# One way to take a mean: replacing the two-matmul norm sums by one-column matmuls in a conformer and attention trunk

## The chip, the cores and the metric

The kernel runs on one core of a Trainium2 chip. The metric is the device time of one execution in microseconds (us), the median of several runs. A core has a matrix engine (TensorE, PE in the profile, with its weight loads as PEld), a vector engine (VectorE, DVE), an activation engine (ScalarE, ACT), a general engine (GpSimd, POOL) and SyncE (SP), which here issues most of the DMAs. Each engine has its own instruction stream and works through it in the order written at build time; between engines there are only semaphores.

## The reference

A trunk of two layers over 512 tokens of width 1024, in float32. Each layer is a half-step SwiGLU feed-forward stage, a mixer (layer 0 a Conformer convolution, layer 1 a sparse attention), a second half-step feed-forward stage, and a gated embedding of a per-layer input p (ple). Each of the four starts with an RMS norm, and one more stands at the end.

```python
def rms_norm(x, g):
    xf = x.astype(jnp.float32)
    y = xf * lax.rsqrt(jnp.mean(xf * xf, axis=-1, keepdims=True) + RMS_EPS)
    return (y * g.astype(jnp.float32)).astype(x.dtype)

def swiglu(x, wg, wu, wd):
    return (jax.nn.silu(x @ wg) * (x @ wu)) @ wd

for i in range(DEPTH):                      # DEPTH = 2
    x = x + 0.5 * swiglu(rms_norm(x, ffn1_norm[i]), ffn1_w_gate[i], ffn1_w_up[i], ffn1_w_down[i])
    h = rms_norm(x, mix_norm[i])
    x = x + (conformer_conv(h, ...) if i % 2 == 0 else nsa_mixer(h, ...))
    x = x + 0.5 * swiglu(rms_norm(x, ffn2_norm[i]), ffn2_w_gate[i], ffn2_w_up[i], ffn2_w_down[i])
    gate = jax.nn.sigmoid(rms_norm(x, ple_norm[i]) @ ple_w_gate[i])
    x = x + gate * (p[i] @ ple_w_in[i])
return rms_norm(x, final_norm)
```

The width of a feed-forward stage is 2816.

## The kernel before

**Layout.** The activations are kept transposed: `self.xs[k]`, k = 0 to 7, each hold 128 of the 1024 channels as partitions and the 512 tokens as columns. Weights arrive in units of 128 x 1024 floats, loaded by SP into `raw` (or `rawx`) tiles of which there are two each. Every float32 operand of a product is split into a high half (`h`, a copy in a reduced format, made by ACT) and a low half (`l`, the difference, made by DVE or POOL): for weights these are `wh` and `wl` (L280, L281), for activations the pairs made in `parts` (L387, L388). A product is three matmuls: `mm3` (L329 to L331) computes high x high, high x low and low x high. All products accumulate in eight PSUM banks.

**The norm.** The norm's gain goes into the activation's split; the norm's factor r, one number for each token, is applied after the matmuls to their result, since it is the same for all channels. So a stage's matmuls can start before r is known. `square_sum` squares each of the eight tiles on ACT and adds them up on DVE in `acc` (L404), 128 partitions x 512 tokens. What remains is a sum over the 128 partitions for each token, a small addition of 1e-6, a power of -0.5 (on POOL, `rsqrt`, L410), and the spreading of r over the 128 partitions, which PE does by four transposes (`spread_raw`, L442) with a copy by ACT to `R` (L449).

`rfin` makes these steps as a generator with two stops: the first `next(fin)` writes down everything to r, the second one the spread. It has two ways of summing over the partitions:

- `soon=True`, used by the two mixers (`conv`, `cmp_in`): `token_sums` (L417) makes four matmuls with 128 columns of `acc` as the stationary operand and one column of 1/1024 as the moving one. The result has the tokens as partitions, 128 x 4. Each of the four float32 matmuls is two instructions in the trace.
- `soon=False`, used by the four feed-forward stages (`ffn`) and the two gates (`ple`): `acc` is split into `h` (ACT, L457) and `l` (DVE, L458), two tiles of the small ring of work tiles (`tmp`, four of them in these stages). `token_means` multiplies a 128 x 128 matrix of 1/1024 by both (L434, two 512-wide matmuls), which gives the mean of every token on every partition, and `diagonal` reads the wanted 128 x 4 numbers out of the bank by four multiply-and-reduce operations with the identity on DVE (L426, each with a read of its accumulator). Then comes the addition (L436).

**A feed-forward stage.** The 22 tiles of the hidden width go in three parts (`PARTS`). The first two tiles (f = 0 and 1) are computed plainly: eight products for the gate, eight for the up half each. From f = 2 on the gate of two tiles is computed together by `gate_pair`, with seven products of half size in the place of eight; these need sums and differences of weight blocks (`combine`, L292 to L304, on DVE and ACT) and of activation blocks. The latter are made once a stage by `right_sums`, called four times (two calls after f = 0, two after f = 1): two scaled copies by ACT (L482), four differences of 256 columns on DVE, and for two results a copy by ACT (L492) and a difference on DVE (all DVE ones at L484). It uses four work tiles a call; its results are the `px` tiles. The third of the seven products is the first to read them.

The calls of `fin` in `ffn`: the first after the products of f = 0, the second between the gate and the up products of f = 1. The multiplications by `R` (L575) come behind f = 1.

**What sets the order.** The order on each engine's stream is chosen at build time by a planner: it follows the order in which the program writes the instructions, but takes a later instruction when it reckons that an earlier one isn't ready yet. `tc.high_priority(100)` (`FIN_PRI`) lets what is written in its block count as written 100 instructions earlier. `tc.issue_after(ins)` demands that what its block writes on the engine of `ins` stands behind `ins` in that engine's stream; it adds no wait for its end. `conv` uses it already to put the tap building of POOL behind the power. `self.root` there is the power's instruction.

Of the kernel before, what the change touches and what calls it, by code (L numbers as in the profile page):

```python
# [11 lines left out]
F32 = mybir.dt.float32  # L12
F32R = mybir.dt.float32r
I32 = mybir.dt.int32
AF = mybir.ActivationFunctionType
OP = mybir.AluOpType
# [10 lines left out]
FIN_PRI = 100  # L27
# [158 lines left out]
class Kern:  # L186
# [230 lines left out]
                self.nc.tensor.matmul(p[:, q:q + 1], t[:, q * 128:q * 128 + 128], self.mean[:, :1],  # L417
                                      start=n == 0, stop=n == len(tiles) - 1)

    def diagonal(self, src, tag, n=4):  # L420

        nc = self.nc
        v = self.tiny.tile([128, 4], F32, name=tag, tag=tag)[:, :n]
        junk = self.cpool.tile([128, 128], F32, name="junk", tag="junk", bufs=1)
        for q in range(n):
            nc.vector.tensor_tensor_reduce(out=junk, in0=src[:, q * 128:q * 128 + 128], in1=self.ident, scale=1.0,  # L426
                                           scalar=0.0, op0=OP.mult, op1=OP.add, accum_out=v[:, q:q + 1])
        return v

    def token_means(self, acc, eps):  # L430
        nc = self.nc
        p = self.bank()
        for n, t in enumerate(acc):
            nc.tensor.matmul(p, self.meanr, t, start=n == 0, stop=n == 1)  # L434
        v = self.diagonal(p, "v")
        nc.vector.tensor_scalar(v, v, eps, None, op0=OP.add)  # L436
        return self.rsqrt(v, 4)

    def spread_raw(self, r, n=4):
        p = self.bank()[:, :n * 128]  # L440
        for q in range(n):
            self.nc.tensor.transpose(p[:, q * 128:q * 128 + 128], r[:, q:q + 1].to_broadcast([128, 128]), self.ident)  # L442
        return p
# [5 lines left out]
        nc.scalar.activation(R, p, AF.Copy)  # L449
        return R  # L450

    def rfin(self, acc, soon=False):


        if not soon:
            h, l = self.tmp(F32R), self.tmp(F32R)
            self.nc.scalar.activation(h, acc, AF.Copy)  # L457
            self.nc.vector.tensor_tensor(l, acc, h.bitcast(F32), op=OP.subtract)  # L458

        def steps():  # L460
            with self.tc.high_priority(FIN_PRI):
                if soon:
                    p = self.bank()[:, :4]
                    self.token_sums(p, [acc])
                    v = self.tiny.tile([128, 4], F32, name="v", tag="v")
                    self.nc.vector.tensor_scalar(v, p, 1e-6, None, op0=OP.add)
                    r = self.rsqrt(v, 4)
                else:
                    r = self.token_means((h, l), 1e-6)
            yield  # L470
            self.R = self.spread(r)
            yield

        return steps()


    def right_sums(self, name, i, k):
# [58 lines left out]
    def ffn(self, n, i, nxt):  # L536
        nc = self.nc
        X = self.X
        g, u, d = (f"ffn{n}_w_{s}" for s in ("gate", "up", "down"))
        self.now, self.T4 = (g, i), []  # L540
        fin = self.rfin(self.acc)

        def plain(p, nm, f, ks=range(KD)):
            for k in ks:
                self.mm3(p, self.block((nm, i, k, f)), X[k], k == 0, k == KD - 1)

        for pi, fs in enumerate(PARTS):
            hid = {}

            def gated(f, gr, pu):  # L550
                nc.vector.tensor_tensor(pu, pu, gr, op=OP.mult)  # L551
                h, l = self.ptile("hid", HIDS, dt=F32R), self.ptile("hid", HIDS, dt=F32R)
                nc.scalar.activation(h, pu, AF.Copy)
                nc.vector.tensor_tensor(l, pu, h.bitcast(F32), op=OP.subtract)
                hid[f] = (h, l)

            if pi == 0:
                assert PLAIN == 2
                wait = []
                for f in range(PLAIN):  # L560
                    pg, pu = self.bank(), self.bank()
                    for ks in (range(KD - 1), (KD - 1,)) if f == 0 else (range(KD),):
                        plain(pg, g, f, ks)
                        if f == 1:
                            next(fin)
                        plain(pu, u, f, ks)
                    wait.append((f, pg, pu))
                    if f == 0:
                        next(fin)
                    for k in (2 * f, 2 * f + 1):  # L570
                        self.right_sums(f"ffn{n}_norm", i, k)
                R = self.R
                for f, pg, pu in wait:
                    gr = self.tmp()
                    nc.vector.tensor_tensor(pg, pg, R, op=OP.mult)  # L575
                    nc.scalar.activation(gr, pg, AF.Silu)
                    gated(f, gr, pu)
            for f in fs[::2]:
                if f < PLAIN:
                    continue  # L580
                G = self.gate_pair(g, i, f)
                nc.vector.tensor_tensor(G, G, R[:, None, :].to_broadcast([128, 2, 512]), op=OP.mult)
                nc.scalar.activation(G, G, AF.Silu)
                for h in range(2):
                    p = self.bank()
                    plain(p, u, f + h)
                    gated(f + h, G[:, h], p)
                self.skew_next()
                self.skew_next()
            last = pi == len(PARTS) - 1  # L590
            if last:
                self.prep_start(*nxt)
            for ms in ((0, 1), *((m,) for m in range(2, KD))):
                p = {m: self.bank() for m in ms}
                if len(ms) > 1:
                    self.held = {ENTRY[PLACE[d, i, f, m][0]] for f in fs for m in ms}
                for part in (fs[:-2], fs[-2:]):
                    for m in ms:
                        for f in part:
                            self.mm3(p[m], self.block((d, i, f, m)), hid[f], f == fs[0], f == fs[-1])  # L600
                self.held = set()
                for m in ms:
                    nc.vector.scalar_tensor_tensor(p[m], p[m], 0.5, R, op0=OP.mult, op1=OP.mult)  # L603
                    nc.vector.tensor_tensor(self.xs[m], p[m], self.xs[m], op=OP.add)
                    if last:
                        self.prep(m)
# [192 lines left out]
    def conv(self, nxt):  # L799

        nc = self.nc
# [3 lines left out]
        self.dwc = self.phase.tile([128, KD, TAPS], F32, name="dwc")  # L805
        nc.gpsimd.dma_start(self.dwc, self.a["dwc"])
        self.ud, self.yd = (self.dpool.tile([D, S], F32, name=n) for n in ("ud", "yd"))
        fin = self.rfin(self.acc, True)
        self.T, self.late, self.done, self.mid, self.squares, self.sqp = {}, [], [], None, None, SQP
        work = {"dve": self.dw_dve, "pool": self.dw_pool, "pe": self.dw_pe}  # L810
        queues = {on: [] for on in work}
# [63 lines left out]
        with self.tc.high_priority(FIN_PRI):  # L875
# [4 lines left out]
            v = self.tiny.tile([128, 4], F32, name="v", tag="v")  # L880
# [3 lines left out]
            r = self.rsqrt(v, 4)  # L884
# [7 lines left out]
        for c in range(KD):  # L892
            pair = self.ptile("tw", TWB, 128 * LAGS, F32R)
            h, l = pair[:, :512], pair[:, 512:1024]
# [144 lines left out]
    def cmp_in(self, j, first):  # L1039

        nc = self.nc
        KC, wait = {}, []
        if first:
            fin = self.rfin(self.acc, True)
        for gp in range(2):
            p = self.bank()
            for k in range(KD):
                self.mm3(p, self.block(("nsa_w_in", 0, k, ("c", j, gp))), self.X[k], k == 0, k == KD - 1)
            wait.append((gp, p))
            if first and gp == 0:  # L1050
                next(fin)
        if first:
            self.proj_gates()
            next(fin)
        for gp, p in wait:
            for s in range(2):
                t = self.ptile("e", EB, 516)
                o = 1 - s
                sl, ot = slice(s * 64, s * 64 + 64), slice(o * 64, o * 64 + 64)
                nc.vector.tensor_tensor(t[sl, o:o + 512], p[sl], self.R[sl], op=OP.mult)  # L1060
                nc.sync.dma_start(t[ot, s:s + 512], t[sl, o:o + 512])
                KC[gp * 2 + s] = t
        B = []
        for q4 in range(4):
            b = self.slot()
            bv = b[:, :496].rearrange("p (a n) -> p a n", a=4)
            for g in range(G):
                src = KC[g][:, 1:1 + 512].rearrange("p (c q e) -> p q c e", q=8, e=2)
                pp0 = q4 * 4
                in0 = src[:, pp0 % 8:pp0 % 8 + 4, pp0 // 8:pp0 // 8 + NC, 0]  # L1070
                nc.gpsimd.tensor_tensor(bv[:, :, g * NC:g * NC + NC], in0,
                                        self.pos[:, j, pp0:pp0 + 4, None].to_broadcast([128, 4, NC]), op=OP.add)
            B.append(bv)
        return B
# [400 lines left out]
```

## Time and profile before

| | |
|---|---|
| runs | 2115.99, 2112.11, 2112.36 us; median 2112.36 |
| the profiled execution's own time | 2111.71 us |
| its span | 2109.9 us |
| mean granted TensorE clock | 0.983 |
| norms with the two-matmul sums, sums of squares done at | 19.4 us (first feed-forward stage), 586.8 (second), 951.4 (ple), 1000.6 (third feed-forward stage), 1695.8 (fourth), 2054.0 (ple) |
| norms with one-column sums, the same | 380.7 us (convolution), 1363.2 (attention) |
| HBM read, written | 203.25 MB, 16.29 MB |

How to read the profile's rows. A row of a timeline is: start and duration in us, engine, line of the kernel, operation, output tile <- input tiles, shapes, count, and in brackets how long the engine had been idle and what released it. A row of stretches is: the stretch, its length, busy time of PE, PEld, DVE, ACT and POOL with the number of instructions in brackets, then the granted clock of TensorE as a share of the full one, the busy share of the DMA engines and GB/s. A row of waits is: who waited for whom, us in total, times, the longest in us. A row of a line's instructions gives the shortest, the middle and the longest duration in ns, and when the first and the last one started. A row of groups gives count, busy us and mean ns. Matmuls overlap, so the pace of a stream of them is read from the distance of their starts.

### The profile page before, as it was taken

Reading aid. Unit: us, or ns where it says so; the run is one execution under the profiler, and the core shown is the slowest. Engines: PE = TensorE matmul, PEld = TensorE weight load, DVE = VectorE, ACT = ScalarE, POOL = GpSimd, SP = SyncE. Lnnn points to the kernel's source line nnn. Section 1 sums busy time; section 2 is a strip of 40 time slices with the busy share of each in tenths; the row PEclk is TensorE's granted clock in tenths of the full one; section 3 lists DMA queues with packets and bytes.
Section 4 is the critical chain, followed back from the end, with each engine's and each line's share of the span. In section 5 each row is a group of like instructions: output and inputs, shape, how many; then the busy total and the mean of one; then the engine's idle time right before and its main releaser. Section 6 shows DMA issues by size and latency. Waiting matters only on the chain.

```text
span 2109.9 us, 29020 instructions
## 1 busy us (share of the span) xinstructions
PE 2041.1 (97%) x11048; PEld 1762.0 (84%) x11048; DVE 1431.8 (68%) x2538; ACT 937.9 (44%) x1538; POOL 382.0 (18%) x388
## 2 busy tenths in 40 slices
PE   7999999999989999999899999999999989999998
PEld 6888888888768898988788989787888768898987
DVE  8757566796576665666856656646989785675664
ACT  6424234653553242345532423326888653242343
POOL 0000000785200000021000000446666200000022
PEclk8999999999999999999999999999999999999999
DMA  4323323344273233243233323454333133332241
GB/s 162 111 89 100 101 80 104 94 132 162 90 200 121 80 105 96 81 147 102 80 110 90 110 83 97 155 163 111 86 86 101 36 100 100 94 107 90 90 140 50
DMA packets 77339, 223.52 MB, mean 106 GB/s; under 512 B 8624, under 2 KB 16592, under 8 KB 77200
## 3 DMA queue, kind: packets, MB, share of 16 engines
q1 hardware_dynamic: 76208, 219.26, 33.9%
q0 software_dynamic: 848, 2.34, 0.3%
q8 instruction: 87, 1.43, 0.3%
q14 instruction: 52, 0.43, 0.1%
q10 hardware_dynamic: 144, 0.07, 0.0%
HBM read 203.25 MB, written 16.29 MB: 104 GB/s over the span
## 4 chain that ended last, share of the span: by engine, by line
PE 63%; DVE 6%; ACT 3%; issue 2%; DMA 1%; POOL 0%; SPq 0%; POOLq 0%; DVEq 0%; ACTq 0%
PE b L329 20%; PE b L330 20%; PE b L331 20%; PE b L1144 1%; DVE t L1209 1%; PE b L1206 1%; PE b L1083 1%; ACT e L1164 1%; DVE s L388 1%; PE b L1225 0%; ACT t L1208 0%; PE b L1226 0%; DVE wl L281 0%; ACT ec L1164 0%; DVE e L1162 0%
## 5 line engine op out<-in xcount | busy, mean ns | idle before, releaser
L329 PE MATMUL b<-s,wh 128*128 128x512 f32 (+1 forms) x1568 | 566.6, 362 | 4.5 <-ACT s L387 3.4
L330 PE MATMUL b<-s,wh 128*128 128x512 f32 (+1 forms) x1568 | 565.3, 361 | 1.7 <-DVE s L388 1.4
L331 PE MATMUL b<-s,wl 128*128 128x512 f32 (+1 forms) x1568 | 563.9, 360 | 0.0
L280 ACT ACTIVATE wh<-raw 128x1024 fp32r<-128x1024 f32 (+1 forms) x291 | 306.7, 1055 | 574.9 <-PE b L330 425.5
L281 DVE TENSOR_TENSOR wl<-raw,wh 128x1024 fp32r<-128x1024 f32 (+1 forms) x245 | 306.9, 1254 | 70.7 <-ACT wh L280 64.8
L329 PEld LDWEIGHTS b<-s,wh 128*128 128x128 f32 x1568 | 299.5, 191 | 49.2 <-ACT s L387 5.1
L330 PEld LDWEIGHTS b<-s,wh 128*128 128x128 f32 x1568 | 299.5, 191 | 44.1 <-DVE s L388 2.6
L331 PEld LDWEIGHTS b<-s,wl 128*128 128x128 f32 x1568 | 299.0, 191 | 42.6
L331 PE MATMUL b<-hid,wl 128*128 128x512 f32 x704 | 274.0, 389 | 0.0
L330 PE MATMUL b<-hid,wh 128*128 128x512 f32 x704 | 274.0, 389 | 0.0
L329 PE MATMUL b<-hid,wh 128*128 128x512 f32 x704 | 273.3, 389 | 0.0
L281 POOL TENSOR_TENSOR wl<-raw,wh 128x1024 fp32r<-128x1024 f32 (+1 forms) x53 | 126.6, 2392 | 721.7 <-ACT wh L280 711.7
L329 PE MATMUL b<-px,wh 128*128 128x256 f32 (+1 forms) x632 | 190.1, 301 | 0.0
L331 PE MATMUL b<-px,wl 128*128 128x256 f32 (+1 forms) x632 | 189.9, 301 | 0.0
L330 PE MATMUL b<-px,wh 128*128 128x256 f32 (+1 forms) x632 | 189.8, 301 | 0.0
L603 DVE SCALAR_TENSOR_TENSOR b<-b,R 128x512 f32<-128x512 f32 x96 | 66.5, 697 | 174.4 <-PE b L331 174.4
L330 PEld LDWEIGHTS b<-hid,wh 128*128 128x128 f32 x704 | 132.2, 188 | 27.4
L331 PEld LDWEIGHTS b<-hid,wl 128*128 128x128 f32 x704 | 132.2, 188 | 27.4
L329 PEld LDWEIGHTS b<-hid,wh 128*128 128x128 f32 x704 | 132.2, 188 | 27.4
L551 DVE TENSOR_TENSOR b<-b,G 128x512 f32<-128x512 f32 x80 | 55.7, 698 | 113.7 <-PE b L331 113.7
L329 PEld LDWEIGHTS b<-px,wh 128*128 128x128 f32 x632 | 120.7, 191 | 5.6
L330 PEld LDWEIGHTS b<-px,wh 128*128 128x128 f32 x632 | 120.7, 191 | 5.7
(251 smaller groups left out, 3176.3 us busy)
## 6 DMA issues: line engine op xcount, KB each, us to landing
raw<-in_w SPq DMA_DIRECT2D x295, 512.0 KB, 3.6
rawx<-in_w SPq DMA_DIRECT2D x40, 512.0 KB, 3.6
skew<-table SPq DMA_DIRECT2D x16, 320.0 KB, 10.4
z<-t SPq DMA_DIRECT2D x16, 256.0 KB, 2.1
hid<-z SPq DMA_DIRECT2D x16, 256.0 KB, 4.0
tt<-skew SPq DMA_DIRECT2D x16, 256.0 KB, 2.8
wr<-in_w SPq DMA_DIRECT2D x8, 512.0 KB, 3.9
q<-t SPq DMA_DIRECT2D x32, 128.0 KB, 2.5
```

Of the source, the lines that this page charges most:

```text
L280: nc.scalar.activation(h[:, c], t[:, c], AF.Copy)
L281: eng.tensor_tensor(l[:, c], t[:, c], h[:, c].bitcast(F32), op=OP.subtract)
L329: mm(out, sh, mh, start=start, stop=False)
L330: mm(out, sh, ml, start=False, stop=False)
L331: mm(out, sl, mh, start=False, stop=stop)
L388: nc.vector.scalar_tensor_tensor(view(l), x, g, view(h.bitcast(F32)), op0=OP.mult, op1=OP.subtract)
L551: nc.vector.tensor_tensor(pu, pu, gr, op=OP.mult)
L603: nc.vector.scalar_tensor_tensor(p[m], p[m], 0.5, R, op0=OP.mult, op1=OP.mult)
L1083: nc.tensor.matmul(P[mh][:, :124], w, B[kk // 4][:, kk % 4, :], start=kk == 0, stop=kk == 15)
L1144: nc.tensor.matmul(p[:, :32 - lo + nk], Q, KT[:, i, "sw".index(b), lo:32 + nk], start=i == 0, stop=i == 1)
L1164: nc.scalar.activation(dst, dst, AF.Exp, scale=-1.0, bias=mn[:, a, bi:bi + 1], accum_out=sm[:, a, bi:bi + 1])
L1206: nc.tensor.transpose(p[:, a * 128:a * 128 + 128], J[a, b][:, kt * 128:kt * 128 + 128], self.ident)
```

## The change

`diagonal` and `token_means` are removed; `rfin` has only the way of the one-column sums, and makes no `h` and `l`. The addition's instruction is kept in `self.vins`. The spread is now written under the high priority too, at all eight norms. In `ffn` the calls of `right_sums` stand in `tc.issue_after(self.vins)`: on DVE, whose instruction the addition is, the block sums come behind it; their ACT copies are not bound by it. The two mixers only drop the argument.

```diff
-    def diagonal(self, src, tag, n=4):
-
-        nc = self.nc
-        v = self.tiny.tile([128, 4], F32, name=tag, tag=tag)[:, :n]
-        junk = self.cpool.tile([128, 128], F32, name="junk", tag="junk", bufs=1)
-        for q in range(n):
-            nc.vector.tensor_tensor_reduce(out=junk, in0=src[:, q * 128:q * 128 + 128], in1=self.ident, scale=1.0,
-                                           scalar=0.0, op0=OP.mult, op1=OP.add, accum_out=v[:, q:q + 1])
-        return v
-
-    def token_means(self, acc, eps):
-        nc = self.nc
-        p = self.bank()
-        for n, t in enumerate(acc):
-            nc.tensor.matmul(p, self.meanr, t, start=n == 0, stop=n == 1)
-        v = self.diagonal(p, "v")
-        nc.vector.tensor_scalar(v, v, eps, None, op0=OP.add)
-        return self.rsqrt(v, 4)
...
-    def rfin(self, acc, soon=False):
-
-
-        if not soon:
-            h, l = self.tmp(F32R), self.tmp(F32R)
-            self.nc.scalar.activation(h, acc, AF.Copy)
-            self.nc.vector.tensor_tensor(l, acc, h.bitcast(F32), op=OP.subtract)
-
-        def steps():
-            with self.tc.high_priority(FIN_PRI):
-                if soon:
-                    p = self.bank()[:, :4]
-                    self.token_sums(p, [acc])
-                    v = self.tiny.tile([128, 4], F32, name="v", tag="v")
-                    self.nc.vector.tensor_scalar(v, p, 1e-6, None, op0=OP.add)
-                    r = self.rsqrt(v, 4)
-                else:
-                    r = self.token_means((h, l), 1e-6)
-            yield
+    def rfin(self, acc):
+
+        with self.tc.high_priority(FIN_PRI):
+            p = self.bank()[:, :4]
+            self.token_sums(p, [acc])
+            v = self.tiny.tile([128, 4], F32, name="v", tag="v")
+            self.vins = self.nc.vector.tensor_scalar(v, p, 1e-6, None, op0=OP.add).ins
+            r = self.rsqrt(v, 4)
+        yield
+        with self.tc.high_priority(FIN_PRI):
             self.R = self.spread(r)
-            yield
-
-        return steps()
+        yield
...
                     if f == 0:
                         next(fin)
-                    for k in (2 * f, 2 * f + 1):
-                        self.right_sums(f"ffn{n}_norm", i, k)
+                    with self.tc.issue_after(self.vins):
+                        for k in (2 * f, 2 * f + 1):
+                            self.right_sums(f"ffn{n}_norm", i, k)
...
-        fin = self.rfin(self.acc, True)
+        fin = self.rfin(self.acc)
...
-            fin = self.rfin(self.acc, True)
+            fin = self.rfin(self.acc)
```

## The prediction

> **What bounds the kernel now.** I read the page's head, then the table of who waited for whom, then the timeline around each norm.
>
> ```profile
> span 2109.9 us, 29020 instructions
> PE 2041.1 (97%) x11048; PEld 1762.0 (84%) x11048; DVE 1431.8 (68%) x2538; ACT 937.9 (44%) x1538; POOL 382.0 (18%) x388
> PE b L442 <- POOL r L410: 38.7, 6, 9.1
> ```
>
> TensorE (PE) sets the end: it is busy for 97% of the span, so only what stops or slows PE counts. Its largest single cause of waiting is the spread of the norm's factor r (L442): 38.7 us in six waits. The timeline shows which.
>
> ```profile
> 36.65 1.12 PE L442 MATMUL b<-ident,r 128*128 128x128 f32 x4 [6.64 <-POOL r L410]
> ...
> 530.47 0.54 PE L442 MATMUL b<-ident,r 128*128 128x128 f32 x3 [2.92 <-POOL r L410]
> ...
> 608.88 1.12 PE L442 MATMUL b<-ident,r 128*128 128x128 f32 x4 [9.01 <-POOL r L410]
> ...
> 1017.34 1.12 PE L442 MATMUL b<-ident,r 128*128 128x128 f32 x4 [9.09 <-POOL r L410]
> ...
> 1711.91 1.11 PE L442 MATMUL b<-ident,r 128*128 128x128 f32 x4 [9.11 <-POOL r L410]
> ```
>
> Four of them open the four feed-forward stages, called A to D in this order: 6.64 + 9.01 + 9.09 + 9.11 = 33.85 us. The one at 530 us is the convolution's LayerNorm, which the change leaves alone. With the four it makes 36.77, and only 1.93 us are left for all the rest: the norms of the two per-layer gates (ple) and the two mixers hold PE hardly at all. After each of the four the granted clock (third number from the end of a row) is low:
>
> ```profile
> 36.65:39.97 3.32, 3.32 (x10) 2.79 (x11) 2.61 (x5) 1.93 (x4) 0.00 (x0) 0.53 0.30 118
> 608.88:613.21 4.33, 4.33 (x13) 3.56 (x14) 3.57 (x7) 2.97 (x5) 0.00 (x0) 0.50 1.05 272
> 1008.25:1017.34 9.09, 0.00 (x1) 0.01 (x1) 9.09 (x22) 6.96 (x10) 1.38 (x1) 0.74 0.32 81
> 1017.34:1022.89 5.55, 5.55 (x15) 4.54 (x16) 3.67 (x9) 3.60 (x6) 0.00 (x0) 0.51 0.43 152
> 1711.91:1715.78 3.87, 3.87 (x12) 3.22 (x12) 2.37 (x5) 2.38 (x4) 0.00 (x0) 0.51 0.60 215
> 531.00:535.00 4.00, 4.00 (x13) 3.17 (x12) 3.84 (x7) 2.29 (x4) 0.00 (x0) 0.57 0.25 100
> ```
>
> Lost to the clock: 3.32 x 0.47 + 4.33 x 0.50 + 5.55 x 0.49 + 3.87 x 0.49 = 1.56 + 2.17 + 2.72 + 1.90 = 8.35 us. So at most 33.85 + 8.35 = **42.2 us** stand behind this norm. The third row is C's wait itself: PE 0.00, VectorE (DVE) 9.09 of 9.09. PE waits because DVE, which runs in order, is full. C's chain:
>
> ```profile
> 999.87 0.68 DVE L404 TENSOR_TENSOR acc<-acc,t 128x512 f32<-128x512 f32 x1
> ...
> 1007.15 0.40 PE L434 MATMUL b<-t,meanr 128*128 128x512 f32 x1
> 1007.38 0.39 PE L329 MATMUL b<-s,wh 128*128 128x512 f32 x1
> ...
> 1007.58 0.29 DVE L426 CUSTOM_DVE_ANT_0 junk<-b,ident 128x128 f32<-128x128 f32 x1 [0.20 <-PE b L434]
> ...
> 1015.66 0.16 DVE L436 TENSOR_SCALAR v<-v 128x4 f32<-128x4 f32 x1
> ...
> 1015.90 1.38 POOL L410 TENSOR_TENSOR r<-v,power 128x4 f32<-128x4 f32 x1 [48.76 <-DVE v L436]
> ```
>
> The sum of squares is done at 1000.55, its second matmul goes only at 1007.15 (it needs the low half l, a DVE product), and from the first diagonal read at 1007.58 to v at 1015.66 pass 8.1 us for four reads and an addition: block sums and weight splits sit between them.
>
> **The change part by part.** The mean now comes from eight one-column instructions, as the mixers already have it:
>
> ```profile
> 383.43 0.95 PE L417 MATMUL b<-meanr,acc 128*128 128x1 f32 x8
> 384.24 0.48 PE L330 MATMUL b<-s,wh 128*128 128x512 f32 x1
> ...
> 384.66 1.04 POOL L410 TENSOR_TENSOR r<-v,power 128x4 f32<-128x4 f32 x1 [1.90 <-DVE v L466]
> ```
>
> *PE, six norms.* Eight instructions take 384.24 - 383.43 = 0.81 us of the queue; the two 512-wide ones that go take 1007.38 - 1007.15 = 0.23 each. That adds 0.4 us a norm, **2.4 us** in all, on PE's path and hidden by nothing.
>
> *DVE, six norms.* L458 and four diagonal reads go; the addition stays.
>
> ```profile
> L458 DVE TENSOR_TENSOR t<-acc,t x6: 683/691/693, 23.6 to 2054.7; 128x512 fp32r<-128x512 f32 x6
> L426 DVE CUSTOM_DVE_ANT_0 junk<-b,ident x24: 281/286/292, 29.3 to 2060.6; 128x128 f32<-128x128 f32 x24
> L426 DVE DVE_READ_ACCUMULATOR2_ANT v<- x24: 81/83/84, 29.6 to 2060.8; 128x1 f32 x24
> ```
>
> 0.69 + 4 x (0.286 + 0.083) = 2.2 us a norm. At the two ple norms that is worth nothing: PE doesn't wait there, other matmuls cover it. At A to D it shortens the queue that PE waits for. The ScalarE copy L457 goes too; ScalarE is 44% busy and holds nobody here. Two work tiles (h and l, of four) come free for the block sums.
>
> *The order on DVE.* The block sums (right_sums) go behind the addition to v. Behind that wait stand these, and behind them the first gate product that reads them:
>
> ```profile
> L484 DVE TENSOR_TENSOR t<-t,t x48: 411/419/428, 27.5 to 1719.3; 128x256 f32<-128x256 f32 x48
> L484 DVE TENSOR_TENSOR px<-t,px x32: 679/684/693, 28.6 to 1720.9; 128x512 fp32r<-128x512 f32 x32
> L484 DVE TENSOR_TENSOR t<-t x16: 415/420/427, 26.6 to 1718.2; 128x256 f32<-128x256 f32 x16
> L482 ACT ACTIVATE t<-s,small 128x512 f32<-128x512 f32 x32 | 22.4, 710 | 12.1 <-DVE t L484 12.1
> L492 ACT ACTIVATE px<-t 128x512 fp32r<-128x512 f32 x32 | 19.2, 621 | 12.3 <-DVE t L484 12.3
> ```
>
> Over four stages (64 x 0.419 + 32 x 0.684) / 4 = 12.2 us of DVE a stage. With the sums out of the way, v needs only acc, 0.81 us of PE, and whatever weight work stands before it on DVE. At C, the 8.1 us of reads and the 6.6 us between acc and the second matmul shrink: I take r well before PE's old waiting place at 1008.25, so the wait at L442 is nearly gone (its ends: 0, and the 9.09 of now).
>
> *Where the stall goes.* The block sums have to be ready sooner by what PE gains. The last group's sum against PE's first read of its low half, A to D:
>
> ```profile
> 47.78 1.28 DVE L484 TENSOR_TENSOR px<-t,px 128x512 fp32r<-128x512 f32 x2
> 50.04 0.40 PE L330 MATMUL b<-px,wh 128*128 128x256 f32 x2
> ...
> 619.57 0.68 DVE L484 TENSOR_TENSOR px<-t,px 128x512 fp32r<-128x512 f32 x1
> 620.96 0.28 PE L330 MATMUL b<-px,wh 128*128 128x256 f32 x1
> ...
> 1026.00 1.28 DVE L484 TENSOR_TENSOR px<-t,px 128x512 fp32r<-128x512 f32 x2
> 1029.95 0.28 PE L330 MATMUL b<-px,wh 128*128 128x256 f32 x1
> ...
> 1720.27 1.28 DVE L484 TENSOR_TENSOR px<-t,px 128x512 fp32r<-128x512 f32 x2
> 1723.73 0.28 PE L330 MATMUL b<-px,wh 128*128 128x256 f32 x1
> ...
> 1000.55:1027.20 26.65, 17.56 (x74) 14.32 (x73) 22.95 (x50) 17.53 (x27) 1.38 (x1) 0.81 0.20 59
> ```
>
> The first of each pair of sums ends 0.64 to 0.68 us after its start, so the margins are 1.6, 0.7, 3.3 and 2.8 us. If DVE keeps its order and only loses 2.2 us, what remains of each stall is stall + clock - 0.4 - 2.2 - margin: A 4.0, B 7.9, C 5.9, D 5.6, together 23.4 us. The other end is 0: C's DVE idles 26.65 - 22.95 = 3.7 us of this stretch, weight work for the next pair of gate tiles can go behind the sums, and PE has other matmuls ready that the planner can put first. I take the middle, **11.7 us**, because the idle part alone covers most of C's 5.9 but A and B are fuller. A shorter stall still costs clock: now 8.35 / 33.85 = 0.25 us for each us of stall, so **2.9 us**.
>
> The Trainium skill ("TensorE: Matmul & The Clock Gate", "Why this matters for your kernels") says that PE keeps its full clock through gaps of up to about 3 us; by that the 2.9 would be 0 and the time 2084. The trace doesn't agree: the 2.92 us wait at 530.47 is followed by a granted 0.57, so the row decides.
>
> *The spread is pulled forward* at all eight norms. Too early, PE waits for r: by the row at 384.66 at most r's end, 385.70, less 384.24, or 1.5 us a norm; where it is later than r, as now at the mixers and gates, 0. I take 0, nearest to what those four show.
>
> **Sum.** 42.2 - 2.4 - 11.7 - 2.9 = 25.2 us off the profiled execution's 2111.7 (the runs' median is 2112.4, 0.03% away): **2087 us**.
>
> **The rivals.**
> - *All of it goes.* The planner orders DVE so that no block sum is late: 42.2 - 2.4 = 39.8 us, 2072. For it speak the idle 3.7 us and the freed work tiles; against it the full DVE during each wait.
> - *The wait moves to the gate product.* DVE's order stays, 23.4 us of stall and 5.8 of clock remain: 42.2 - 2.4 - 29.2 = 10.6 us, 2101. For it speak the small margins at A and B.
> - *Nothing measurable.* Splits stay ahead of v, PE waits at L442 as before, less 2.2 us of DVE at each of A to D and plus 2.4 of PE: about 2106 to 2112. Against it: the mixers' v follows its matmuls at once.
> - *Slower: the sums start too late.* Now half of them run before v. Gated, and with four work tiles, the four groups can run one after another: 2 x 0.71 + 4 x 0.42 + 0.62 + 0.68 = 4.4 us each, 17.6 in all, the last low half 1.2 us before that. At C PE would want it at 1029.95 - 9.09 - 2.72 + 0.4 = 1018.5. A stage gains 39.8 / 4 = 10 us on the mean and loses it again when the new stall passes 10 / 1.25 = 8 us; that is the case from v at 1018.5 + 8 - 16.4 = 1010.1 on, 9.5 us after acc. With v at 1012.5: 2.4 x 1.25 x 4 stages = 12 us slower, 2124. Against it: half of the 12.2 us of sums and 1.5 us of reads run ahead of v now; without these 7.6 us it stands at 1015.66 - 7.6 = 1008 or sooner.
>
> **How the numbers follow.** Forecast (2080 to 2097) 0.52; all of it 0.17; moved wait 0.17; nothing 0.06; slower 0.08. The range reaches down to 2072 and up to the moved wait with its slack, 2105; some 0.2 is outside. A measurement tells 0.2% (4 us) from no change: faster 0.86, same 0.06, slower 0.08.
>
> **What would show it.** Right: at A to D no wait over 2 us at L442; v within 8 us of the last L404; DVE without L426; a few us of PE waiting for a DVE px or for a weight product at the first gate pair; a clock near 0.5 for less than 3 us after it. Wrong: L442 still waiting for POOL with DVE full; block sums ending later after acc than C's 26 us; new PE waits at the mixers or gates, where the spread came too early.

## The result, and the profile after

| | before | after |
|---|---|---|
| median of the runs, us | 2112.24 (2111.12 to 2115.99, 4 runs) | 2078.64 (2075.45 to 2082.01, 4 runs) |
| the profiled execution, us | 2111.71 | 2075.45 |
| its span, us | 2109.9 | 2073.7 |
| mean granted clock | 0.983 | 0.993 |

The ratio is 0.9838, with a 95% interval of 0.9816 to 0.986: 33.6 us faster. The forecast was 2087, the range 2072 to 2105.

The head of the page after:

```profile
span 2073.7 us, 29015 instructions
PE 2033.6 (98%) x11084; PEld 1758.6 (85%) x11084; DVE 1424.0 (69%) x2484; ACT 933.5 (45%) x1532; POOL 380.9 (18%) x388
```

Its largest waits of PE (who waited for whom, us in total, times, longest):

```profile
PE b L760 <- DMA uu<-ud: 5.1, 1, 5.1
PE b L329 <- ACT s L387: 5.0, 2, 3.8
PE b L423 <- POOL r L410: 4.8, 2, 2.9
PE b L329 <- ACT px L462: 3.1, 1, 3.1
```

The spread is now line 423 and the block sums are line 454. The spread's wait has fallen from 38.7 us in six to 4.8 in two, and those two are the convolution's LayerNorm (2.92) and the final norm; at A to D there is none. In its place stand one wait of 3.1 us for a block sum, at B, and 5.1 at the convolution's taps, where the timeline before had 2.19. (The row of 5.0 is 3.77 us at the program's start and 1.19 at the attention's norm, where the kernel before had 2.21 and 1.21; at the start the profiles of all kernels lie between 1.71 and 3.77.)

```profile
488.63 0.57 PE L789 MATMUL b<-uu,tw 128*128 128x128 f32 x3 [2.19 <-DMA uu<-ud]
```

The 40 us around each of A to D in the view of stretches (stretch, length, busy us with instructions of PE, its weight loads, DVE, ACT and POOL; granted clock; DMA share; GB/s). Before:

```profile
22.00:62.00 40.00, 33.36 (x182) 28.97 (x182) 35.77 (x66) 22.47 (x32) 1.13 (x1) 0.91 0.26 81
585.00:625.00 40.00, 30.99 (x161) 26.53 (x160) 29.80 (x59) 21.46 (x33) 1.40 (x1) 0.87 0.78 220
1000.00:1040.00 40.00, 30.91 (x167) 26.86 (x166) 34.75 (x66) 23.60 (x35) 1.38 (x1) 0.87 0.22 66
1695.00:1735.00 40.00, 30.37 (x167) 26.17 (x166) 35.34 (x67) 23.90 (x35) 1.40 (x1) 0.87 0.22 67
```

And after:

```profile
22.00:62.00 40.00, 40.00 (x236) 35.52 (x235) 36.50 (x60) 24.40 (x35) 1.48 (x1) 1.00 0.38 116
585.00:625.00 40.00, 36.88 (x203) 31.78 (x202) 27.52 (x50) 19.16 (x30) 1.15 (x1) 1.00 0.79 221
987.00:1027.00 40.00, 40.00 (x230) 35.19 (x229) 33.82 (x57) 24.35 (x36) 1.12 (x1) 1.00 0.27 81
1669.00:1709.00 40.00, 39.68 (x240) 35.15 (x239) 35.60 (x60) 23.45 (x34) 1.14 (x1) 1.00 0.28 93
```

PE was idle for 160 - 125.63 = 34.4 us of these 160 us, and is now for 160 - 156.56 = 3.4. The clock is full in all four. DVE is about as busy as it was (133.4 us against 135.7): its work is nearly the same, and what changed is the order.

C in the timeline after:

```profile
987.12 0.69 DVE L404 TENSOR_TENSOR acc<-acc,t 128x512 f32<-128x512 f32 x1
...
991.92 0.95 PE L417 MATMUL b<-meanr,acc 128*128 128x1 f32 x8
...
992.90 0.16 DVE L439 TENSOR_SCALAR v<-b 128x4 f32<-128x4 f32 x1 [1.90 <-PE b L417]
...
993.15 1.12 POOL L410 TENSOR_TENSOR r<-v,power 128x4 f32<-128x4 f32 x1 [35.37 <-DVE v L439]
...
998.26 0.60 PE L423 MATMUL b<-ident,r 128*128 128x128 f32 x4
...
1009.34 0.28 PE L329 MATMUL b<-px,wh 128*128 128x256 f32 x1
...
1009.46 0.40 PE L329 MATMUL b<-s,wh 128*128 128x512 f32 x1
...
1015.42 0.40 PE L329 MATMUL b<-px,wh 128*128 128x256 f32 x2
...
1016.13 0.40 PE L329 MATMUL b<-s,wh 128*128 128x512 f32 x1
...
1017.63 0.68 DVE L454 TENSOR_TENSOR px<-t,px 128x512 fp32r<-128x512 f32 x1
...
1020.24 0.28 PE L329 MATMUL b<-px,wh 128*128 128x256 f32 x1
```

The addition to v comes 5.1 us after acc is done (987.81 to 992.90), where it took 15.1 (1000.55 to 1015.66). Of the 5.1, 4.1 pass before PE, which runs its own stream in order, comes to the one-column sums (991.92). The spread has no bracket: PE reaches it 4 us after r is there. The last block sum ends at 1018.31, 30.5 us after acc, later than before (26.65), and still nobody waits. From 1009.46 to 1020.24 PE runs 512-wide products of `s` (the up half of the next tiles, 42 of the 48 products that two tiles need), with only a few products of `px` between them: the planner has put work that needs no block sum into the middle of the gate pair. The stretch from 1016.13 to 1020.24 alone covers the end of the last sum.

B, the one place with a remainder:

```profile
591.95 0.69 DVE L292 TENSOR_TENSOR s<-rawx 128x512 f32<-128x512 f32 x1 [6.69 <-DMA rawx<-in_w]
...
614.87 0.69 DVE L292 TENSOR_TENSOR s<-rawx 128x512 f32<-128x512 f32 x1 [5.25 <-DMA rawx<-in_w]
...
618.29 0.39 PE L329 MATMUL b<-px,wh 128*128 128x256 f32 x1 [3.12 <-ACT px L462]
```

Here DVE twice waits for a weight tile. It did so before as well, once before v and once among the block sums:

```profile
594.81 0.69 DVE L292 TENSOR_TENSOR s<-rawx 128x512 f32<-128x512 f32 x1 [6.23 <-DMA rawx<-in_w]
...
616.42 0.69 DVE L292 TENSOR_TENSOR s<-rawx 128x512 f32<-128x512 f32 x1 [3.27 <-DMA rawx<-in_w]
```

So at B v comes 8.6 us after acc in the changed kernel (583.94 to 592.55), behind the first of the two weight waits; before it came 20.4 us after (586.81 to 607.16). The skew tables of the attention are copied on the same SP queue at this time, before and after, and the DMA share in this stretch is 0.79 (0.78 before) against 0.27 to 0.38 in the other three.

### The profile page after: what moved, and what is told of

It is laid out like the page before. It is cut to its first block, busy times and chain, and to the rows that moved or that the text cites. A ratio compares the mean times of both kernels' runs of the same rounds, so it can differ in the third digit from the quotient of the medians.

```text
span 2073.7 us, 29015 instructions
## 1 busy us (share of the span) xinstructions
PE 2033.6 (98%) x11084; PEld 1758.6 (85%) x11084; DVE 1424.0 (69%) x2484; ACT 933.5 (45%) x1532; POOL 380.9 (18%) x388
## 4 chain that ended last, share of the span: by engine, by line
PE 62%; DVE 5%; ACT 3%; DMA 2%; issue 1%; POOL 0%; SPq 0%; POOLq 0%; ACTq 0%; DVEq 0%
PE b L329 19%; PE b L330 19%; PE b L331 19%; DMA raw<-in_w 1%; DMA skew<-table 1%; PE b L1115 1%; DVE t L1180 1%; PE b L1054 1%; PE b L1177 1%; ACT e L1135 1%; DVE s L388 1%; ACT t L1179 0%; PE b L1196 0%; PE b L1197 0%; DVE e L1133 0%
```

## The experiments

Three groups were each run beside the kernel before on one chip; its median there was 2113.75, 2112.88 and 2115.38 us, so kernels of different groups are compared by their ratios.

| kernel | median, us (lowest to highest, runs) | ratio to before, 95% interval |
|---|---|---|
| cols_only | 2076.52 (2069.62 to 2078.12, 4) | 0.9819 [0.98, 0.9839] |
| gate_only | 2101.64 (2100.89 to 2104.98, 4) | 0.9948 [0.9933, 0.9963] |
| cols_gate | 2074.51 (2071.58 to 2075.88, 4) | 0.9814 [0.98, 0.9829] |
| no_fill | 2115.62 (2113.93 to 2118.17, 10) | 1.0007 [0.9998, 1.0017] |
| after_again | 2076.55 (2075.08 to 2077.03, 5) | 0.9827 [0.9813, 0.9841] |
| table_copies_held | 2073.87 (2072.6 to 2076.04, 4) | 0.9815 [0.9802, 0.9829] |
| sums_twice | 2090.15 (2089.3 to 2091.55, 4) | 0.9892 [0.9878, 0.9906] |
| cols_spread | 2080.63 (2077.99 to 2081.18, 5) | 0.9843 [0.9829, 0.9857] |
| reads_kept | 2103.85 (2098.6 to 2108.61, 4) | 0.9946 [0.9925, 0.9966] |
| split_kept | 2095.41 (2093.23 to 2096.27, 4) | 0.9905 [0.9891, 0.9918] |
| gates_old | 2078.49 (2078.23 to 2079.31, 4) | 0.9827 [0.9814, 0.9841] |
| best | 2071.34 (2069.25 to 2072.7, 5) | 0.9792 [0.9779, 0.9805] |

### Which part of the change does it

The change has three parts: the one-column sums, the demand that the block sums stand behind the addition, and the spread pulled forward. `cols_only` keeps the first alone:

```diff
-                    with self.tc.issue_after(self.vins):
-                        for k in (2 * f, 2 * f + 1):
-                            self.right_sums(f"ffn{n}_norm", i, k)
+                    for k in (2 * f, 2 * f + 1):
+                        self.right_sums(f"ffn{n}_norm", i, k)
...
-        with self.tc.high_priority(FIN_PRI):
-            self.R = self.spread(r)
+        self.R = self.spread(r)
```

> The changed kernel without the other two edits: the one-column sums at all eight norms, but the block sums free to stand ahead of the addition, and the spread written where it was. Theory 1 (DVE's queue as a whole held r: four diagonal reads, the low half and the block sums): the addition is one instruction instead of five, so r comes some us sooner than before, but block sums still stand ahead of it; waits for r of 1 to 5 us are left at A to D and the time is 2085 to 2100. Theory 2 (the sums alone do it): 2079, as the whole change. Theory 3 (the order of the block sums alone does it): 2110, as before.

`gate_only` is the kernel before with the demand alone, behind its own addition:

```diff
-        nc.vector.tensor_scalar(v, v, eps, None, op0=OP.add)
+        self.vins = nc.vector.tensor_scalar(v, v, eps, None, op0=OP.add).ins
...
-                    for k in (2 * f, 2 * f + 1):
-                        self.right_sums(f"ffn{n}_norm", i, k)
+                    with self.tc.issue_after(self.vins):
+                        for k in (2 * f, 2 * f + 1):
+                            self.right_sums(f"ffn{n}_norm", i, k)
```

> The kernel before with one edit: the block sums of the feed-forward stages stand behind the old addition on DVE; the two-matmul sums and the diagonal reads stay. Theory 1: the low half and the second matmul stay late (6.6 us after acc at C), the reads then follow each other without block sums between, r is 3 to 6 us sooner than before: 2090 to 2102. Theory 3 (the order alone does it): 2079 to 2083. Theory 2 (the sums alone do it): 2112. If the gate only starves DVE while it waits for the second matmul, block sums are late at the gate products and the time is 2112 to 2125.

`cols_gate` is the changed kernel with the spread where it was (the second part of the first diff), `cols_spread` the changed kernel without the demand (the first part of it).

> The changed kernel with the spread no longer pulled forward. In the changed kernel the spread stands 3 to 5 us behind the end of r at A, C and D, about where it stood before. If pulling it forward matters only for the mixers and gates, where PE didn't wait before either, the time is that of the changed kernel, 2076 to 2082. If it is what frees the PSUM banks and the work tiles early, 2085 or more.

> The changed kernel without the demand that block sums stand behind the addition; the spread stays pulled forward. With the one-column sums alone the time was 2076.5 already. Theory 2 (the sums do it, the order of block sums adds nothing since the planner places the addition early by its priority): that of the changed kernel within 3 us. Rival (the spread pulled forward needs the order): 2082 or more.

The one-column sums alone give 0.9819, as much as the whole change (0.9838 and, run again, 0.9827). The demand added to them changes nothing that can be told: 0.9819 and 0.9814 without the early spread, 0.9843 and 0.9827 with it. So it is theory 2 that fits, and theory 1's waits at A to D didn't stay. `cols_gate` lies 1.5 us below its expected range, and `cols_spread` 4.1 us above the changed kernel run again, where at most 3 had been expected: pulling the spread forward looks like a loss of 2 to 4 us, though the intervals overlap (more in the last part of this section). The demand by itself gives 12 us of the 34. C in `gate_only` shows why it isn't enough:

```profile
995.00 0.69 DVE L404 TENSOR_TENSOR acc<-acc,t 128x512 f32<-128x512 f32 x1
...
1002.28 0.40 PE L434 MATMUL b<-t,meanr 128*128 128x512 f32 x1
...
1007.29 0.16 DVE L436 TENSOR_SCALAR v<-v 128x4 f32<-128x4 f32 x1
...
1008.71 1.11 PE L442 MATMUL b<-ident,r 128*128 128x128 f32 x4 [5.33 <-POOL r L410]
```

No block sum stands ahead of v any more, but weight splits do: between acc and the second matmul 6.6 us, and from there to v another 5.0. Waits of 5.16, 1.86, 5.33 and 5.35 stay at A to D, 17.7 of the 33.85 us.

### What made r late: the low half or the four reads

Both variants start from `cols_only` and change the six norms of the feed-forward stages and gates (`soon` is true at the mixers alone). `reads_kept` drops the split and keeps the reads (`diagonal` is put back):

```diff
-            p = self.bank()[:, :4]
-            self.token_sums(p, [acc])
...
+            if soon:
+                p = self.bank()[:, :4]
+                self.token_sums(p, [acc])
+            else:
+                b = self.bank()
+                nc = self.nc
+                nc.tensor.matmul(b, self.meanr.bitcast(F32), acc, start=True, stop=True)
+                p = self.diagonal(b, "v")
```

> The kernel with the one-column sums alone (no demand on the block sums, the spread not pulled forward), but at the six norms of the feed-forward stages and the gates the mean is again made for all partitions by one 512-wide float32 product straight from acc (two instructions), with the four diagonal reads on VectorE behind it. The split into a high and a low half is gone, the reads are kept. Before, C lost 6.6 us between acc and the second matmul and 8.1 us from the first read to v, and its wait was 9.1 us. Theory 1 (the strung-out reads are the larger cause): of the 33.85 us at A to D a wait of 2 to 6 us each stays at the spread, 10 to 22 us with the clock; beside the 2076.5 of one-column sums alone that is 2087 to 2098. Theory 2 (the late low half was the larger cause): under 2 us of wait at each, 2077 to 2082.

`split_kept` drops the reads and keeps the split:

```diff
+        if not soon:
+            h, l = self.tmp(F32R), self.tmp(F32R)
+            self.nc.scalar.activation(h, acc, AF.Copy)
+            self.nc.vector.tensor_tensor(l, acc, h.bitcast(F32), op=OP.subtract)
+        return self.rsteps([acc] if soon else [h.bitcast(F32), l.bitcast(F32)])
+
+    def rsteps(self, acc):
...
-            self.token_sums(p, [acc])
+            self.token_sums(p, acc)
```

> The same kernel with the one-column sums, but at those six norms acc is again split into h (ScalarE) and l (VectorE), and the one-column sums are taken over both, so sixteen instructions in the place of eight and v behind the low half; the reads are gone. Theory 1: what the split alone makes late is small, waits at the spread of under 2 us at A to D; with the second eight instructions at six norms (0.8 to 1.7 us each, 5 to 10 us) 2081 to 2088. Theory 2 (the late low half was the larger cause): waits of 2 to 6 us each at the spread, 2092 to 2108.

The waits at the spread of A to D in the timeline of `reads_kept`:

```profile
32.07 0.85 PE L433 MATMUL b<-ident,r 128*128 128x128 f32 x4 [2.54 <-POOL r L410]
...
604.27 1.12 PE L433 MATMUL b<-ident,r 128*128 128x128 f32 x4 [4.60 <-POOL r L410]
...
1014.35 0.90 PE L433 MATMUL b<-ident,r 128*128 128x128 f32 x3 [9.87 <-POOL r L410]
...
1706.36 1.11 PE L433 MATMUL b<-ident,r 128*128 128x128 f32 x4 [4.86 <-POOL r L410]
```

These are 21.9 us. In `split_kept` they are 0.90, none, 0.77 and 0.79, 2.5 in all. So the reads, strung out between other work on DVE, cost PE more waiting, and theory 1 is right in what it says of the waits, but for C's 9.87, which is above its 6. But either part alone holds v back: at C it comes 10.0 us after acc with the reads and 8.4 with the split, against 15.1 before and 2.6 in `cols_only`; at D the split is even the later one (7.7 against 6.4). At C PE has other work until 8.1 us after acc in `reads_kept` and 9.0 in `split_kept`, so only what comes later than that makes a wait.

Theory 1's times were not right: `reads_kept` lies above 2087 to 2098 and `split_kept` above 2081 to 2088. In the first, 10.2 us of the waits come from two powers, at C and D, that took 7.67 and 4.81 us in the place of 1.1 (in the last section); 11.7 are left for the reads themselves. Its four runs lie 10 us apart. In the second, these waits came to the spread's 7.3 (4.8 in `cols_only`):

```profile
PE b L423 <- POOL r L410: 7.3, 5, 2.9
PE b L329 <- ACT px L468: 5.4, 3, 4.5
...
PE b L329 <- ACT t L552: 3.1, 2, 1.5
```

(The rows are from its view of waits.) The 5.4 for block sums (4.5 of it at B) stands against a wait of 2.1 at the same place, B, for a copy of the gate pair in `cols_only`, the 3.1 (the first two tiles' gates) against 0.9: 2.5 + 3.3 + 2.2 = 8.0 us more of waiting. Eight more one-column instructions at six norms are 6 x 0.89 = 5.3 (the duration follows below), and a mean clock of 0.989 against 0.991 is about 0.002 x 2094.5 = 4.2 us. That makes 17.5 of the 19.8 us between the two spans (2094.5 and 2074.7).

### Why the residual didn't come

The prediction kept 11.7 us of stall at the first gate pair. If the up products of the next tiles are what hides it, forcing them behind the pair's products should bring it back. `no_fill` is the changed kernel with

```diff
+        self.pairend = self.lastmm
...
-                    plain(p, u, f + h)
+                    if f == PLAIN:
+                        with self.tc.issue_after(self.pairend):
+                            plain(p, u, f + h)
+                    else:
+                        plain(p, u, f + h)
```

where `pairend` is the last instruction of the first gate pair on PE.

> The changed kernel with one demand more: at the first gate pair of each feed-forward stage the up products of its two tiles stand behind the seven gate products on PE, so that PE can't do them while block sums are missing. Theory 1 with filling (the block sums are no sooner than before, and PE doesn't wait because the planner puts 512-wide up matmuls into the gaps; at C some 24 of them, 5.5 us): PE waits 4 to 6 us at each of A to D for a px tile, 2095 to 2105 with the clock. Rival (the block sums are ready in time by themselves since DVE has less to do): 2076 to 2083.

Its waits of PE:

```profile
PE b L329 <- ACT px L462: 16.1, 9, 4.4
...
PE b L329 <- DVE t L481: 3.2, 3, 1.8
...
PE b L330 <- DVE px L454: 2.3, 7, 0.6
```

PE now waits 21.6 us for block sums and for what follows the gate products, close to the 23.4 that the prediction had as its upper end, and the whole gain is gone (1.0007); the time lies 11 us above the expected range. With the fill 3.1 us stay. The block sums themselves are no later: at C the last one ends 28.7 us after acc, against 30.5 in the changed kernel, and at A, B and D it differs by 1.4 us at most. The prediction's residual was there; it was covered by up products.

### The remainder at B, the mean's own cost, and the gates

`after_again` is the changed kernel once more. `table_copies_held` holds each skew copy on SP behind the last weight load issued:

```diff
-            self.nc.sync.dma_start(t[:, c], self.a["w"][j, :, c])
+            self.load = self.nc.sync.dma_start(t[:, c], self.a["w"][j, :, c]).ins
...
-            self.nc.sync.dma_start(self.skew[h][:, :640], self.table[h:h + 1, :].to_broadcast([128, 640]))
+            with self.tc.issue_after(self.load):
+                self.nc.sync.dma_start(self.skew[h][:, :640], self.table[h:h + 1, :].to_broadcast([128, 640]))
```

> The changed kernel itself, to stand beside the others on one chip. Its four runs so far fell on two levels, 2075 to 2076 with a mean granted clock of 0.993 and 2081 to 2082 with 0.990. If the levels come from half-clock stretches after short PE waits that happen in some executions and not in others, each run's time follows its mean clock, some 2 us for each 0.001; if they come from something else, the two levels have the same clock.

> The changed kernel with the 16 copies of the bias table (skew, 320 KB each, needed only in the attention of layer 1) each put on SP's queue behind the weight load written last before it, instead of all at once at the start of stage B. Theory: in B, DVE waits 6.7 and 5.25 us for weight DMAs that share the queue with these copies, and PE waits 3.1 us for block sums behind them; spread out, both go: 2071 to 2075, and the runs lie closer together. Rival (the weight loads at B are late for another reason, or the wait moves to the up products): 2076 to 2082.

The five runs of `after_again` don't fall on two levels, and their times don't follow the clock (0.993 at 2076.55 us, 0.991 at 2075.08): what the two levels of the first four runs were stays open.

B's wait, 1.79 in `after_again` and 3.12 in the changed kernel, is not in the profile with the copies held, and DVE's waits for weight tiles between 575 and 625 us are 6.3 us in the place of 10.7; this fits the late weight tile as its cause, but it rests on one profile of each. The time is 2.7 us lower, but the intervals (0.9802 to 0.9829 and 0.9813 to 0.9841) overlap.

`sums_twice` makes the one-column sums twice at all eight norms:

```diff
             self.token_sums(p, [acc])
+            self.token_sums(p, [acc])
```

> The changed kernel with the one-column sums made twice into the same bank at all eight norms: eight more instructions, 0.81 us of PE each time. If they lie on PE's path with nothing hidden, as the prediction says, 8 x 0.81 = 6.5 us more, 2083 to 2087. If they fill gaps in which PE would wait, 2076 to 2080.

The convolution's norm in its timeline:

```profile
375.27 1.84 PE L417 MATMUL b<-meanr,acc 128*128 128x1 f32 x16
```

Sixteen take 1.84 us, eight 0.95: 0.89 more, 7.1 us for eight norms. Measured are 13.6. Beside them B's wait for a block sum rose from 1.79 to 5.40 and that for the attention's kt from 1.07 to 2.24, and the mean clock fell from 0.991 to 0.989 (about 0.002 x 2089 = 4 us): 7.1 + 3.6 + 1.2 + 4 = 15.9, against 15.7 between the spans of the two profiled executions (2089.0 and 2073.3). Here time put ahead of v cost more than its own length, and more than the 2087 expected at most. How much of the surplus belongs to it is not shown: B's wait is 3.12 in one profile of the changed kernel and 1.79 in the other.

`gates_old` puts the old way back at the two gates.

> The changed kernel, with the two-matmul sums and the diagonal reads put back at the two per-layer gates only. The prediction takes these two norms as worth nothing, apart from 0.4 us of PE each: 2076 to 2080, as the changed kernel. Rival: the shorter chain helps there too (the second gate stands near the end of the program), 2081 to 2087.

It takes 2078.49 us, its ratio is that of the changed kernel run again (0.9827): the two gates' norms are worth nothing that can be told, either way.

### The best of the parts

The tap wait of the convolution was 5.0 to 5.2 us in all seven profiles with the early spread; without it, it was 2.00 to 2.69 in six (the kernel before among them) and 4.32 in `reads_kept`. `best` is the changed kernel with the spread where it was and the copies held.

> The changed kernel with the spread written where it was (not pulled forward) and each skew table copy behind the last weight load on SP's queue. If both readings hold (the early spread costs the convolution 2 to 3 us by a later tap wait, the copies cost B 2 to 3 us of late weights), the convolution's tap wait is 2.0 to 2.7 us instead of 5.1 and B has no wait over 1.5 us: 2069 to 2073. Rival: the planner's order shifts other waits in their place, and it stays at 2073.5 to 2077.

The tap wait in its timeline:

```profile
481.80 3.36 PE L759 MATMUL b<-uu,tw 128*128 128x128 f32 x28 [2.47 <-POOL tw L651]
```

The tap wait is 2.47, B has none, and the time is 2071.34, a ratio of 0.9792. Its interval lies below that of the changed kernel in both its measurements, so it beats both kernels; against `cols_gate` and `table_copies_held`, which have one of the two edits each, the intervals overlap. How the early spread delays the taps, through the planner's order of the products that feed them, was not followed.

## Why the prediction was right, and where it was off

- **The bound and its size.** Right. The 33.85 us at the spread of A to D are gone, and so are the 8.35 us of low clock behind them (the two tables of stretches). The reading of the bound was made at C and taken for all four; at B DVE was not full the whole time but stood 6.23 us for a weight tile between acc and v. Small besides: the copy L457, said to hold nobody, held PE for 0.5 us at D.
- **Which operations made r late.** Right: the reads and the split together. The reads alone leave 21.9 us of waiting (11.7 without the two slow powers), the split alone 2.5; in time the two lie closer, by the ratios some 27 and 18 us above `cols_only`. The block sums ahead of v, which the prediction took out as well, decide little once the reads are gone: without the demand the time is the same.
- **PE, 2.4 us.** Not contradicted: the eight take 0.81 us of the queue, 0.95 with the end. The prediction took it as PE's time alone; doubling the sums cost 13.6 / 8 = 1.7 us a norm, with the waits and the clock of that run.
- **The two gates at nothing.** Right (`gates_old`).
- **The residual stall: the mis-sized term.** The prediction took the middle of 0 and 23.4 us, 11.7, and 2.9 of clock for it. Measured are 3.1 us at B and a full clock. It named the cover itself ("PE has other matmuls ready that the planner can put first") but gave it no size. It could have: the up products of two tiles stand ready and need no block sum, and at C they fill the greater part of 1009.46 to 1020.24, where C's residual was reckoned at 5.9. (42 products, 0.227 us from one start to the next, are 9.5 us.) A and D came out at 0 where 4.0 and 5.6 were reckoned, C at 0 too, and at B the 7.9 became 3.1, behind the weight tile's DMA, which the prediction didn't look at. It took B for fuller than C on DVE; the stretches before show the opposite, 29.80 us busy of 40 against 34.75, because of the two weight waits. The full clock is that of one profile: in `after_again` B's wait is 1.79 us and the 4 us behind it (616.21 to 620.21) have a clock of 0.57, 1.7 us lost.
- **The spread pulled forward at 0.** Off by one step: PE doesn't wait for r at the mixers, as said, but the convolution's tap wait is 2.9 us longer (5.09 against 2.19), and in the 4 us behind it the clock is 0.63 (484.21 to 488.21), where it was 1.00 before (488.63 to 492.63): another 1.5 us.
- **The sum again.** 42.2 - 2.4 - 3.1 - 2.9 = 33.8 us, against 36.3 between the two profiled executions and 33.6 between the medians. Of the 36.3, 28.7 are idle time of PE (68.8 and 40.1 us) and 7.5 its busy time; the 2.5 us that the sum lacks were not traced further.
- **The rivals.** "All of it goes" (2072) is nearest to what happened at A to D; `best` reaches it. "The wait moves to the gate product" is what `no_fill` shows, and it is dearer than the 2101 reckoned for it: the clock takes as much as the stall. Its span is 39.6 us longer than the changed kernel's (2113.3 and 2073.7): 21.6 - 3.1 = 18.5 us of waiting, and a mean clock of 0.985 against 0.993, about 0.008 x 2113.3 = 17 us, where 0.25 us for each us of stall had been put. "The sums start too late" asked for v 9.5 us after acc at C; it came after 5.1.
- **The sign that misled.** "Block sums ending later after acc than C's 26 us" was to show it wrong. They end after 30.5, and it costs nothing: that sign looked at DVE and not at whether PE had something else. One sign of being right was missed by a little: v was to come within 8 us of acc, and at B it took 8.6.
- **The clock's rule.** The prediction set one row (0.57 after the 2.92 us wait) against the page "TensorE: Matmul & The Clock Gate" of the Trainium skill. One row was too little. The same wait of 2.92 us stands at the same matmul in all fourteen profiles. Over the 4 us that begin half a us behind the start of this matmul, the clock is 0.57 to 0.59 in eight of them, the kernel before and the changed kernel among them, and 1.00 in the other six. In the view of stretches, in the changed kernel (matmul at 527.45):

```profile
528.00:532.00 4.00, 4.00 (x12) 3.13 (x12) 3.87 (x7) 3.14 (x5) 0.00 (x0) 0.57 0.33 118
```

and in `best` (matmul at 523.65):

```profile
524.20:528.20 4.00, 4.00 (x19) 3.23 (x19) 3.86 (x7) 3.14 (x5) 0.00 (x0) 1.00 0.60 192
```

Once the clock falls (0.57, as before the change), once it stays (1.00, as the page's rule has it). A wait of 2.92 us is worth a chance here, not a price.

## What to carry to other kernels

When a wait is taken away, look at what the waiting engine could do at the place where the wait would turn up next, and put a length to it: ready work of the same engine covers a late operand, and here it was worth as much as the whole change. A small result that others wait for should be made by instructions that stand together in their queue: four reads strung out among other work on DVE made it late, where eight instructions in a row on PE, the busiest engine, didn't. Then ask which transfer the earlier work now runs into.

## What was not expected of the hardware

**The power on POOL can end long after it starts when DVE is busy.** For four columns it takes 1.0 to 1.5 us in most places, 1.9 or 2.6 in a few. In `reads_kept` two took far more, and so did one in `cols_spread`. C and D in the timeline of `reads_kept`, with the last DVE row ahead of the power's end:

```profile
1006.63 7.67 POOL L410 TENSOR_TENSOR r<-v,power 128x4 f32<-128x4 f32 x1 [43.65 <-DVE v L455]
...
1012.20 1.23 DVE L281 TENSOR_TENSOR wl<-raw,wh 128x1024 fp32r<-128x1024 f32 x1
...
1701.49 4.81 POOL L410 TENSOR_TENSOR r<-v,power 128x4 f32<-128x4 f32 x1 [44.56 <-DVE v L455]
...
1704.72 0.69 DVE L295 TENSOR_TENSOR raw<-raw 128x512 f32<-128x512 f32 x1
```

The power at C ends at 1014.30, 0.87 us after DVE's unbroken work (1013.43); that at D at 1706.30, 0.89 after 1705.41. In `cols_spread` it is the same:

```profile
994.67 5.41 POOL L410 TENSOR_TENSOR r<-v,power 128x4 f32<-128x4 f32 x1 [35.72 <-DVE v L439]
...
998.79 0.41 DVE L454 TENSOR_TENSOR t<-t 128x256 f32<-128x256 f32 x1
```

1000.08 less 999.20 is 0.88. The Trainium skill ("SBUF — State Buffer", "Who interferes with whom") says that DVE and POOL share a pair of ports under an exclusive lock, and that a DVE instruction with two inputs in SBUF contends with a POOL instruction that reads SBUF. The rows agree in kind: wherever DVE works during a power of four columns, in all the profiles, the power ends 0.87 to 0.91 us after the end of one of DVE's instructions. Elsewhere that is the first, second or third one; here it is the eleventh at C, the eighth at D and the ninth in `cols_spread`. That the power waits for its turn at the ports is a reading of this; why it came so late three times stays open, and no run set out to test it.

**The clock after a short wait differs from profile to profile.** The attention's norm holds PE for 1.2 and 0.5 us in every kernel. The 10 us that begin 1.0 us behind the start of the first matmul after it, in the changed kernel:

```profile
1341.00:1351.00 10.00, 10.00 (x47) 7.83 (x48) 0.67 (x2) 1.06 (x1) 9.64 (x11) 1.00 0.79 266
```

and those 0.4 us behind it in `sums_twice`:

```profile
1347.00:1357.00 10.00, 9.51 (x35) 7.78 (x35) 1.33 (x3) 1.16 (x2) 7.42 (x11) 0.66 0.84 264
```

Over the fourteen profiles the granted clock of this stretch is 1.00 twice, 0.83 seven times and 0.66 five times. The last takes 10 x 0.34 = 3.4 us from a run, which is of the size by which runs of one kernel differ here (1 to 10 us).
